# First norm's scale and shift spread by float32r products on four row groups, and one low weight part made on GpSimd

## The chip, the core and the metric

The kernel runs on one core of one Trainium2 chip. The metric is the device time of one launch in microseconds (us); lower is better. A core has five engines that work side by side and wait for one another by semaphores: TensorE (PE in the profile; PEld is its weight load), VectorE (DVE), ScalarE (ACT), GpSimd (POOL) and SyncE (SP), which here only issues transfers.

## What is computed

The reference is a trunk of two encoder layers over 512 tokens of width 1024. A layer norm stands ahead of the first layer, and the change is around that norm:

```python
def layer_norm(x, g, b):
    xf = x.astype(jnp.float32)
    mu = jnp.mean(xf, axis=-1, keepdims=True)
    var = jnp.mean(jnp.square(xf - mu), axis=-1, keepdims=True)
    return ((xf - mu) * lax.rsqrt(var + LN_EPS)).astype(x.dtype) * g + b
...
def hybrid_layer(x, w_in, ...):
    hcat = x @ w_in + b_in
    ...
    p_a = (y_a * jax.nn.silu(na_z)) @ w_br_a   # neighbourhood attention
    p_b = (y_b * jax.nn.silu(gq_z)) @ w_br_b   # grouped-query attention
    p_c = (y_c * jax.nn.silu(sg_z)) @ w_br_c   # spatial gating
    merged = g[:, :, 0] * p_a + g[:, :, 1] * p_b + g[:, :, 2] * p_c
    return layer_norm(DEEPNORM_ALPHA * x + merged @ w_out + b_out, ln_g, ln_b)
...
    h = layer_norm(x, ln_in_g, ln_in_b)
    for l in range(DEPTH):
        h = hybrid_layer(h, w_in[l], ...)
```

## The kernel before, in words

Tokens lie in four tiles of 128 rows. Every matrix product is made of three float32r products: each operand is split into a high part (a copy to float32r, on ScalarE) and a low part (the operand minus its high part), and high x high, low x high and high x low are summed in PSUM. Weights are split in the same way, 512 KB at a time.

`first_layer_start` (from L320) is the start of the program. It stands in `in_order`, which chains the instructions of each engine in the order in which they are written, so nothing in it is moved by a scheduler. Its work:

- SyncE issues the loads on its queue: token tile 0, weight parts q0 and q1, tile 1, q2, q3, tile 2, k0, tile 3, k1. Each is 512 KB. q0 to q3 are the query columns of the input projection (256 rows of depth each), k0 and k1 the key and value columns. Behind them come the constants (L99 to L104, L273 to L275).
- ScalarE's queue carries two loads: `lnrow`, the norm's scale g and shift b as one row of 2048 numbers on partition 0, and `ident`, the 64 KB identity for transposes.
- TensorE spreads that row over all partitions (L347): a column of ones on one partition times half a row of g or b gives a 128x512 tile in PSUM, once for each of g and b and each half, so four products in float32. The results are `gains[j, h]` (`lnb` in the profile; j is 0 for g, 1 for b; h the half).
- `stats(i)` makes a tile's mean and variance on VectorE (L223 to L225) and the power -0.5 on GpSimd (L226). `apply(i)` (L356) makes the normed tile in four VectorE steps, L359 and L361 for each half, then 4 + 4 transposes on TensorE (L365, `xt_in`), and ScalarE and VectorE split the transposed tile into `xh` and `xl` (L249, L250). Tile 0 reads `gains` from PSUM; the other tiles read `lnc`, ScalarE's copy of it in SBUF (L388).
- `high(n)` is a weight part's high copy on ScalarE (L337), `low(n, engine)` its low part on the named engine (L340): q0 and q1 on GpSimd, q2 and q3 on VectorE, k0 on GpSimd, k1 on VectorE.
- `gq_queries(0, i)` (L306) is the query product of tile i: 24 products, in six quartets. The first three quartets read q0 and q1 (high parts with `xh`, high with `xl`, low with `xh`), the last three q2 and q3 in the same way. `gq_keys_values(0, i)` (L196 to L198) follow from tile 0 on.

So the last quartet of `gq_queries(0, 0)` needs the low parts of q2 and q3; behind it on TensorE stand the transposes of tile 1, and behind them `gq_queries(0, 1)`.

After the start comes the planned part: a list of steps (`run_steps`) in which each projection's weights are loaded, split and used, up to the second layer's output.

Of the kernel before, what the change touches and what calls it, by code (L numbers as in the profile page):

```python
# [9 lines left out]
F32 = mybir.dt.float32  # L10
F32R = mybir.dt.float32r
AF = mybir.ActivationFunctionType
ALU = mybir.AluOpType
# [4 lines left out]
P = 128  # L18
D = 1024
KD = D // P  # L20
S = 512
# [31 lines left out]
def tile_encoder(ctx: ExitStack, tc: tile.TileContext, a, out):  # L53
    nc = tc.nc
    scalar = nc.scalar
# [14 lines left out]
    act = nc.scalar.activation  # L70
    dve = nc.vector
    pool = nc.gpsimd
    pe = nc.tensor

    cst = ctx.enter_context(tc.tile_pool(name="cst", bufs=1))
    wp = ctx.enter_context(tc.tile_pool(name="wp", bufs=2))
    rp = ctx.enter_context(tc.tile_pool(name="rp", bufs=8))
# [8 lines left out]
    pw = cst.tile([P, 10], F32, name="pw")  # L86
    pool.memset(pw, -0.5)

    one = cst.tile([P, 1], F32, name="one")
    pool.memset(one, 1.0)  # L90
    bcol = cst.tile([P, DEPTH, NCOL], F32, name="bcol")
    hcol = cst.tile([P, DEPTH, NCOL], F32, name="hcol")
    bvg = cst.tile([P, DEPTH, NKV], F32, name="bvg")
# [20 lines left out]
    def psum(tag, name):  # L114
        return pp.tile([P, S], F32, tag=tag, name=name, bufs=3 if tag == "acc" else 5)

    def t2(name):
        return tp.tile([P, S], F32, tag="t2", name=name, bufs=4)
# [4 lines left out]
    def asf(r):  # L123
        return r.bitcast(F32)
# [4 lines left out]
    def input_load(i):  # L129
        xi = st["xin", i] = t4(f"xin_{i}")  # L130
        nc.sync.dma_start(xi, a["x"][P * i:P * i + P, :])

    def load(src, nk, ncol, name):
        if name in ("gq0_0", "gq0_1", "gq0_2"):
            raw = fp.tile([P, nk, ncol], F32, tag="f8", name=f"raw_{name}")
        else:
            raw = wp.tile([P, nk, ncol], F32, tag="raw", name=f"raw_{name}", bufs=3)
        nc.sync.dma_start(raw, src.rearrange("(k p) c -> p k c", p=P))
        return raw
# [77 lines left out]
    def row_stats(src, n, name, wide=512):  # L217
        bs = sp.tile([P, 4, 6], F32, tag="st", name=f"st_{name}")
        mv = sp.tile([P, 2], F32, tag="mv", name=f"mv_{name}")
        rs = sp.tile([P, 1], F32, tag="rs", name=f"rs_{name}")  # L220
        nb = n // wide
        for j in range(nb):
            dve.bn_stats(bs[:, j, :], src[:, wide * j:wide * j + wide])  # L223
        dve.bn_aggr(mv, bs[:, 0:nb, :])
        dve.tensor_scalar(out=rs, in0=mv[:, 1:2], scalar1=LN_EPS, scalar2=None, op0=ALU.add)  # L225
        st["pow"] = pool.tensor_tensor(rs, rs, pw[:, 0:1], op=ALU.pow).ins  # L226
        return mv, rs
# [18 lines left out]
    def split_x(ps, i, b):  # L246
        pv = ps.rearrange("p (j t) -> p j t", t=P)
        hi = xh[:, 4 * b:4 * b + 4, P * i:P * i + P]
        act(hi, pv, AF.Copy)  # L249
        st["xl"] = dve.tensor_tensor(xl[:, 4 * b:4 * b + 4, P * i:P * i + P], pv, asf(hi), op=ALU.subtract).ins  # L250
# [37 lines left out]
    def gqw_tile(name):  # L288
        w = rp.tile([P, 2, 2, S], F32R, tag="r8", name=f"w_{name}")
        return w[:, 0], w[:, 1]  # L290
# [8 lines left out]
    def gq_queries(l, i):  # L299
        ps = st["psq", i] = psum("att", f"gq_{l}_{i}")  # L300
        tk = slice(P * i, P * i + P)
        w = [[st["gqw", k // 2][p][:, k % 2] for k in range(KD)] for p in range(2)]
        for k0 in range(0, KD, 4):
            for n, (x, p) in enumerate(((xh, 0), (xl, 0), (xh, 1))):
                for k in range(k0, k0 + 4):
                    pe.matmul(ps, lhsT=x[:, k, tk], rhs=w[p][k], start=n + k == 0, stop=n == 2 and k == KD - 1)  # L306

    def gq_keys_values(l, i):
        if i % 2 == 0:
            st["pskv", i // 2] = psum("acc", f"gkv_{l}_{i // 2}")  # L310
        ps = st["pskv", i // 2][:, 256 * (i % 2):256 * (i % 2) + 256]
        tk = slice(P * i, P * i + P)
        for k in range(KD):
            whi, wlo = st["kvw"][k // 4]
            mm3(ps, xh[:, k, tk], xl[:, k, tk], whi[:, k % 4], wlo[:, k % 4], k == 0, k == KD - 1)
# [3 lines left out]
    def first_layer_start():  # L319
        raw = {}  # L320
        input_load(0)
        rows = rp.tile([P, 2, D], F32, tag="r8", name="lnrow")[0:1]
        scalar.dma_start(rows, a["ln_in_rows"])
        scalar.dma_start(ident, a["ident"])
        for n in ("q0", "q1", 1, "q2", "q3", 2, "k0", 3, "k1"):
            if isinstance(n, int):
                input_load(n)
            else:
                raw[n] = load(*(gqw_spec if n[0] == "q" else kvw_spec)(0, int(n[1])))
        w = {}  # L330

        def high(n):
            if n[0] == "q":
                w[n] = gqw_tile(f"gq0_{n[1]}")
            else:
                w[n] = [wp.tile([P, 4, 256], F32R, tag=t, name=f"{t}_gkv0_{n[1]}") for t in ("whi", "wlo")]
            act(w[n][0], raw[n], AF.Copy)  # L337

        def low(n, engine):
            engine.tensor_tensor(w[n][1], raw[n], asf(w[n][0]), op=ALU.subtract)  # L340

        gains = {}
        lnc = st["lnc"] = cst.tile([P, 2, D], F32, tag="cvec", name="lnc_in")
        for h in range(2):
            for j in range(2):
                ps = gains[j, h] = psum("acc" if h + j < 2 else "att", f"lnb_{h}_{j}")
                pe.matmul(ps, lhsT=one[0:1].broadcast_to([1, P]), rhs=rows[:, j, 512 * h:512 * h + 512],  # L347
                          start=True, stop=True)

        def stats(i):  # L350
            st["stats", i] = row_stats(st["xin", i], D, f"in{i}")

        def apply(i):
            xi, (mv, rs) = st["xin", i], st["stats", i]
            xt = []
            for h in range(2):  # L356
                cs = slice(512 * h, 512 * h + 512)
                g, b = [gains[j, h] if i == 0 else lnc[:, j, cs] for j in range(2)]
                dve.scalar_tensor_tensor(out=xi[:, cs], in0=xi[:, cs], scalar=mv[:, 0:1], in1=g,  # L359
                                         op0=ALU.subtract, op1=ALU.mult)  # L360
                dve.scalar_tensor_tensor(out=xi[:, cs], in0=xi[:, cs], scalar=rs, in1=b, op0=ALU.mult, op1=ALU.add)  # L361
                ps = psum("att", f"xt_in{i}_{h}")
                for j in range(4):
                    c = 512 * h + P * j
                    pe.transpose(ps[:, P * j:P * j + P], xi[:, c:c + P], ident)  # L365
                xt.append(ps)
            for h in range(2):
                split_x(xt[h], i, h)
            if i:
                scalar.dma_start(hbuf[0][i], xi)  # L370

        stats(0)
        high("q0")
        low("q0", pool)
        high("q1")
        low("q1", pool)
        apply(0)
        high("q2")
        low("q2", dve)
        stats(1)  # L380
        high("q3")
        low("q3", dve)
        for kc in range(4):
            st["gqw", kc] = w[f"q{kc}"]
        gq_queries(0, 0)
        for h in range(2):
            for j in range(2):
                act(lnc[:, j, 512 * h:512 * h + 512], gains[j, h], AF.Copy)  # L388
        scalar.dma_start(hbuf[0][0], st["xin", 0])
        apply(1)  # L390
        high("k0")
        low("k0", pool)
        stats(2)
        high("k1")
        low("k1", dve)
        st["kvw"] = w["k0"], w["k1"]
        gq_queries(0, 1)
        gq_keys_values(0, 0)
        apply(2)
        stats(3)  # L400
        gq_keys_values(0, 1)
        gq_queries(0, 2)
        apply(3)
        gq_keys_values(0, 2)
        gq_keys_values(0, 3)
        gq_queries(0, 3)
# [514 lines left out]
    with in_order():  # L921
        first_layer_start()
# [4 lines left out]
    for l in range(DEPTH):  # L927
# [5 lines left out]
        M, R, T = gq_moments, gq_rotate, gq_stack  # L933
# [134 lines left out]
```

## Time and profile before

| | |
|---|---|
| median of 3 runs | 1092.2 us (1090.23 to 1094.16) |
| the profiled execution | 1090.98 us, of which the span in the trace is 1089.2 us |
| TensorE matmul busy | 1075.7 us (99% of the span), 5744 records |
| VectorE busy | 640.5 us (59%) |
| ScalarE busy | 470.6 us (43%) |
| GpSimd busy | 52.8 us (5%), 54 instructions |
| chain that ended last | PE 97%, DVE 2% |

The span begins with the first instruction that the trace holds; the 1.8 us between it and the execution's own time lie around it. Busy time is an average over the whole program. The change is in the first 25 us, so it is read from timelines and waits of that stretch.

### The profile page before, as it was taken

To read this page: it belongs to the slowest core of one execution; us is meant where nothing else is said; L and a number is where in the kernel's file an instruction comes from. 1 tells how busy PE (TensorE), PEld (TensorE's weight loads), DVE (VectorE), ACT (ScalarE), POOL (GpSimd) and SP (SyncE) were. 2 spreads that over 40 slices of the span, in tenths; PEclk is the share of its full clock that TensorE was granted. 3 is DMA by queue.
4 is the path that set the end of the run, shared out by engine and by line. 5 is a ranking of instruction groups with operands and counts; after the bars stand their busy time and mean duration, and the time that the engine had idled before them with its cause. 6 is when DMAs were issued, how large, how long until landed. Compare 5 with 4: busy or idle time off the path is not lost.

```text
span 1089.2 us, 14738 instructions
## 1 busy us (share of the span) xinstructions
PE 1075.7 (99%) x5744; PEld 887.8 (82%) x5744; DVE 640.5 (59%) x1205; ACT 470.6 (43%) x841; POOL 52.8 (5%) x54
## 2 busy tenths in 40 slices
PE   8999999999999999999999999999999999999997
PEld 5988788888888888888888887888888888888886
DVE  6775956665554543546876478566555555344465
ACT  4245735555655422334422365455645643223320
POOL 4420000000000000000021000000000000000001
PEclk9999999999999999999999999999999999999999
DMA  7522322213333433335652332222233334333421
GB/s 284 165 78 82 100 97 59 59 55 91 115 111 117 137 97 97 108 105 174 231 180 58 97 110 73 78 58 58 86 102 87 115 117 135 97 97 97 135 78 58
DMA packets 142808, 116.59 MB, mean 107 GB/s; under 512 B 4881, under 2 KB 130321, under 8 KB 142737
## 3 DMA queue, kind: packets, MB, share of 16 engines
q1 hardware_dynamic: 141872, 113.21, 33.5%
q10 hardware_dynamic: 866, 2.43, 0.6%
q8 instruction: 45, 0.74, 0.3%
q14 instruction: 25, 0.20, 0.1%
HBM read 109.34 MB, written 6.29 MB: 106 GB/s over the span
## 4 chain that ended last, share of the span: by engine, by line
PE 97%; DVE 2%; DMA 0%; issue 0%; ACT 0%; DVEq 0%
PE gq L306 4%; PE gy L735 3%; PE gb L196 3%; PE gc L198 3%; PE gc L197 3%; PE po L198 3%; PE po L197 3%; PE po L196 3%; PE gc L196 3%; PE ga L198 3%; PE ga L196 3%; PE gb L198 3%; PE gb L197 3%; PE ga L197 3%; PE gt L723 3%; PE gs L703 2%
## 5 line engine op out<-in xcount | busy, mean ns | idle before, releaser
L706 DVE TENSOR_REDUCE nm<-gs 128x1 f32<-128x512 f32 x64 | 42.3, 684 | 26.9 <-PE gs L704 26.8
L709 ACT ACTIVATE gp<-gs,nm 128x512 f32<-128x512 f32 x64 | 43.8, 688 | 21.4 <-DVE nm L706 19.8
L198 PE MATMUL gc<-xh,wlo_gc 128*128 128x512 f32 x128 | 51.1, 399 | 0.0
L725 ACT ACTIVATE gpT<-gt 128x512 f32<-128x512 f32 x64 | 36.7, 598 | 31.0 <-PE gt L723 30.8
L197 PE MATMUL gc<-xl,whi_gc 128*128 128x512 f32 x128 | 50.0, 391 | 0.0
L196 PE MATMUL gc<-xh,whi_gc 128*128 128x512 f32 x128 | 50.0, 391 | 0.0
L196 PE MATMUL gb<-xh,whi_gb 128*128 128x512 f32 x128 | 50.0, 391 | 0.0
L198 PE MATMUL gb<-xh,wlo_gb 128*128 128x512 f32 x128 | 49.8, 389 | 0.0
L197 PE MATMUL gb<-xl,whi_gb 128*128 128x512 f32 x128 | 49.8, 389 | 0.0
L196 PE MATMUL ga<-xh,whi_ga 128*128 128x512 f32 x128 | 49.8, 389 | 0.0
L198 PE MATMUL ga<-xh,wlo_ga 128*128 128x512 f32 x128 | 49.8, 389 | 0.0
L197 PE MATMUL ga<-xl,whi_ga 128*128 128x512 f32 x128 | 49.8, 389 | 0.0
L226 POOL TENSOR_TENSOR rs_po<-rs_po,pw 128x1 f32<-128x1 f32 x8 | 7.5, 939 | 814.4 <-DVE rs_po L225 814.4
L143 ACT ACTIVATE whi_gb<-raw_gb 128x1024 fp32r<-128x1024 f32 x16 | 17.0, 1060 | 60.4 <-PE pb L197 22.7
L779 ACT ACTIVATE nt<-nt,mx 128x256 f32<-128x256 f32 x64 | 30.1, 471 | 23.3 <-DVE mx L775 22.7
L144 DVE TENSOR_TENSOR wlo_ga<-raw_ga,whi_ga 128x1024 fp32r<-128x1024 f32 x16 | 19.6, 1222 | 33.5 <-ACT whi_ga L143 33.5
L735 PE MATMUL gy<-gpT,gv 128*64 128x128 f32 x512 | 38.8, 279 | 0.0
L723 PE MATMUL gt<-ident,gp 128*128 128x128 f32 x256 | 37.4, 276 | 0.7 <-ACT gpT L725 0.7
L735 PEld LDWEIGHTS gy<-gpT,gv 128*64 128x64 f32 x512 | 29.6, 136 | 10.2 <-issue 8.3
L144 DVE TENSOR_TENSOR wlo_gb<-raw_gb,whi_gb 128x1024 fp32r<-128x1024 f32 x16 | 19.6, 1222 | 30.1 <-ACT whi_gb L143 29.9
L723 PEld LDWEIGHTS gt<-ident,gp 128*128 128x128 f32 x256 | 29.7, 140 | 8.6 <-issue 2.7
L306 PE MATMUL gq<-w_gq,xh 128*128 128x512 f32 x128 | 34.0, 398 | 0.0
(282 smaller groups left out, 3099.0 us busy)
## 6 DMA issues: line engine op xcount, KB each, us to landing
raw_o<-in_w_out SPq DMA_DIRECT2D x24, 512.0 KB
raw_gc<-in_w_in SPq DMA_DIRECT2D x16, 512.0 KB
raw_gb<-in_w_in SPq DMA_DIRECT2D x16, 512.0 KB
raw_ga<-in_w_in SPq DMA_DIRECT2D x16, 512.0 KB
raw_gq<-in_w_in SPq DMA_DIRECT2D x8, 512.0 KB
raw_sv<-in_w_in SPq DMA_DIRECT2D x8, 512.0 KB
raw_nv<-in_w_in SPq DMA_DIRECT2D x8, 512.0 KB
raw_zb<-in_w_in SPq DMA_DIRECT2D x8, 512.0 KB
```

Of the source, the lines that this page charges most:

```text
L144: dve.tensor_tensor(wlo, raw, asf(whi), op=ALU.subtract)
L196: pe.matmul(ps, lhsT=lhi, rhs=rhi, start=first, stop=False)
L197: pe.matmul(ps, lhsT=lhi, rhs=rlo, start=False, stop=False)
L198: pe.matmul(ps, lhsT=llo, rhs=rhi, start=False, stop=last)
L306: pe.matmul(ps, lhsT=x[:, k, tk], rhs=w[p][k], start=n + k == 0, stop=n == 2 and k == KD - 1)
L703: pe.matmul(ps, lhsT=lhs, rhs=st["ks"][:, g, 0, :], start=True, stop=False)
L706: dve.tensor_reduce(out=nm, in_=ps, axis=AX.X, op=ALU.max, negate=True)
L709: act(pt, ps, AF.Exp, bias=nm, accum_out=sm)
L723: pe.transpose(ps[:, P * k:P * k + P], pt[:, P * k:P * k + P], ident)
L725: act(pT, ps, AF.Copy)
L735: pe.matmul(ps[64 * e:64 * e + 64, P * t:P * t + P], lhsT=st["gv"][:, k, HD * g:HD * g + HD], rhs=st["gp", hp, t, e][:, P * k:P * k + P], ...
L779: act(T[:, cs], T[:, cs], AF.Exp, bias=mx[:, i:i + 1], scale=SCALE, accum_out=sm[:, i:i + 1])
```

## The change

The scale and shift no longer come as one row. A transfer (`lnflat`) writes them to all 128 partitions: a row of 512 numbers to each, the same one to 32 partitions in a row, in the order g first half, b first half, g second half, b second half. The input array is laid out anew on the host for that. ScalarE makes the high part of this tile, GpSimd the low part, and a 32x128 block of 1/32 takes the place of the column of ones. Each `gains[j, h]` is now two float32r products (high, then low) over the 32 partitions that hold its row, so eight products in place of four. The block of 1/32 is filled by a GpSimd memset in the same tile. The second edit makes the low part of q3 on GpSimd in place of VectorE, and puts it ahead of `stats(1)` in the text.

```diff
-    one = cst.tile([P, 1], F32, name="one")
-    pool.memset(one, 1.0)
...
         raw = {}
         input_load(0)
-        rows = rp.tile([P, 2, D], F32, tag="r8", name="lnrow")[0:1]
-        scalar.dma_start(rows, a["ln_in_rows"])
+        rows = rp.tile([P, 3, S], F32R, tag="r8", name="lnrow")
+        one = rows[:, 2, 0:P]
+        pool.memset(asf(one), 1.0 / 32)
+        R = a["ln_in_rows"]
+        flat = t2("lnflat")
+        scalar.dma_start(flat, bass.AP(tensor=R.tensor, offset=R.offset, ap=[[S, 4], [0, 32], [1, S]]))
         scalar.dma_start(ident, a["ident"])
...
         lnc = st["lnc"] = cst.tile([P, 2, D], F32, tag="cvec", name="lnc_in")
-        for h in range(2):
-            for j in range(2):
-                ps = gains[j, h] = psum("acc" if h + j < 2 else "att", f"lnb_{h}_{j}")
-                pe.matmul(ps, lhsT=one[0:1].broadcast_to([1, P]), rhs=rows[:, j, 512 * h:512 * h + 512],
-                          start=True, stop=True)
+        act(rows[:, 0], flat, AF.Copy)
+        pool.tensor_tensor(rows[:, 1], flat, asf(rows[:, 0]), op=ALU.subtract)
+        for p in range(2):
+            for h in range(2):
+                for j in range(2):
+                    q = 64 * h + 32 * j
+                    if p == 0:
+                        gains[j, h] = psum("acc" if h + j < 2 else "att", f"lnb_{h}_{j}")
+                    pe.matmul(gains[j, h], lhsT=one[q:q + 32], rhs=rows[q:q + 32, p],
+                              start=p == 0, stop=p == 1)
...
         high("q2")
         low("q2", dve)
+        high("q3")
+        low("q3", pool)
         stats(1)
-        high("q3")
-        low("q3", dve)
...
-    arrays["ln_in_rows"] = np.ascontiguousarray(np.stack([v["ln_in_g"], v["ln_in_b"]])[None])
+    arrays["ln_in_rows"] = np.ascontiguousarray(np.stack([v["ln_in_g"], v["ln_in_b"]]).reshape(2, 2, S).transpose(1, 0, 2))
```

Of the rest of the program no engine's order is different. Two places move.

GpSimd, from its first memset to the low part of k0, before (`rs_in` is the power of `stats`, `w_gq` the low parts of q0, q1, q3, `wlo_gkv` that of k0):

```order
L87 MEMSET pw 128x10
L90 MEMSET one 128x1
L109 MEMSET nkl 64x512 x2
L226 ISA
L226 TENSOR_TENSOR rs_in_136<-rs_in_136,pw 128x1
L340 TENSOR_TENSOR w_gq_0_142<-raw_gq_0_107,w_gq_0_142 128x1024
L340 TENSOR_TENSOR w_gq_1_145<-raw_gq_1_109,w_gq_1_145 128x1024
L226 TENSOR_TENSOR rs_in_171<-rs_in_171,pw 128x1
L340 TENSOR_TENSOR wlo_gkv_0_230<-raw_gkv_0_119,whi_gkv_0_229 128x1024
```

The same place on GpSimd after the change:

```order
L87 MEMSET pw 128x10
L109 MEMSET nkl 64x512 x2
L324 MEMSET lnrow 128x128
L349 ISA
L349 TENSOR_TENSOR lnrow<-lnflat,lnrow 128x512
L226 TENSOR_TENSOR rs_in_142<-rs_in_142,pw 128x1
L344 TENSOR_TENSOR w_gq_0_148<-raw_gq_0_107,w_gq_0_148 128x1024
L344 TENSOR_TENSOR w_gq_1_151<-raw_gq_1_109,w_gq_1_151 128x1024
L344 TENSOR_TENSOR w_gq_3_175<-raw_gq_3_115,w_gq_3_175 128x1024
L226 TENSOR_TENSOR rs_in_180<-rs_in_180,pw 128x1
L344 TENSOR_TENSOR wlo_gkv_0_236<-raw_gkv_0_119,whi_gkv_0_235 128x1024
```

The low part of the norm's rows now stands ahead of tile 0's power, and the low part of q3 ahead of tile 1's power.

VectorE, from the last step of `apply(0)` to the first of `apply(1)`, before (`lnb` is `gains`, `lnc_in` its copy in SBUF):

```order
L361 SCALAR_TENSOR_TENSOR xin_102<-xin_102,rs_in_136,lnb_1_132 128x512
L250 TENSOR_TENSOR xl<-xt_in_0_150,xh 128x4x128
L250 TENSOR_TENSOR xl<-xt_in_1_157,xh 128x4x128
L340 TENSOR_TENSOR w_gq_2_166<-raw_gq_2_113,w_gq_2_166 128x1024
L223 BN_STATS st_in_169<-xin_111 128x6 x2
L224 BN_AGGR mv_in_170<-st_in_169 128x2
L225 TENSOR_SCALAR rs_in_171<-mv_in_170 128x1
L340 TENSOR_TENSOR w_gq_3_177<-raw_gq_3_115,w_gq_3_177 128x1024
L359 SCALAR_TENSOR_TENSOR xin_111<-xin_111,mv_in_170,lnc_in 128x512
```

The same place on VectorE after the change:

```order
L370 SCALAR_TENSOR_TENSOR xin_100<-xin_100,rs_in_142,lnb_1_134 128x512
L250 TENSOR_TENSOR xl<-xt_in_0_156,xh 128x4x128
L250 TENSOR_TENSOR xl<-xt_in_1_163,xh 128x4x128
L344 TENSOR_TENSOR w_gq_2_172<-raw_gq_2_113,w_gq_2_172 128x1024
L223 BN_STATS st_in_178<-xin_111 128x6 x2
L224 BN_AGGR mv_in_179<-st_in_178 128x2
L225 TENSOR_SCALAR rs_in_180<-mv_in_179 128x1
L368 SCALAR_TENSOR_TENSOR xin_111<-xin_111,mv_in_179,lnc_in 128x512
```

One row is gone from VectorE: q3's low part between the statistics of tile 1 and the first step of `apply(1)`.

## Rows read from the trace of the kernel before

**Rows 1.** Waits of TensorE over the whole span: us in total, times, longest.

```profile
PE lnb L347 <- DMA lnrow<-in_ln_in_rows: 3.5, 1, 3.5
PE xt_in L365 <- DVE xin L361: 1.8, 2, 0.9
```

**Rows 2.** Chain that ended last, 0 to 60 us: start us, us, what.

```profile
0.72 2.67 DMA lnrow<-in_ln_in_rows
...
3.53 7.16 PE lnb L347 x8
...
14.26 1.23 DVE w_gq L340
...
17.04 1.23 DVE w_gq L340
...
20.57 0.76 DVE xin L361
...
22.10 5.49 PE gq L306 x24
```

**Rows 3.** Timeline of TensorE: start us, us, instruction, shapes, count, [idle before].

```profile
12.42 1.80 PE L306 MATMUL gq<-w_gq,xh 128*128 128x512 f32 x4
14.06 1.09 PE L306 MATMUL gq<-w_gq,xl 128*128 128x512 f32 x4
14.98 2.00 PE L306 MATMUL gq<-w_gq,xh 128*128 128x512 f32 x8
...
19.86 0.66 PE L365 MATMUL xt_in<-ident,xin 128*128 128x128 f32 x4 [0.81 <-DVE xin L361]
```

**Rows 4.** Timeline of VectorE.

```profile
4.70 1.29 DVE L223 BATCH_NORM_STATS2 st_in<-xin 128x6 f32<-128x512 f32 x2 [4.70 <-DMA xin<-in_x]
6.33 0.74 DVE L359 SCALAR_TENSOR_TENSOR xin<-xin,mv_in,lnb 128x512 f32<-128x512 f32 x1
10.72 0.75 DVE L361 SCALAR_TENSOR_TENSOR xin<-xin,rs_in,lnb 128x512 f32<-128x512 f32 x1 [0.96 <-PE lnb L347]
25.01 2.24 DVE L340 TENSOR_TENSOR wlo_gkv<-raw_gkv,whi_gkv 128x1024 fp32r<-128x1024 f32 x1
```

**Rows 5.** Timeline of ScalarE.

```profile
6.17 1.06 ACT L337 ACTIVATE w_gq<-raw_gq 128x1024 fp32r<-128x1024 f32 x1 [3.21 <-DMA raw_gq<-in_w_in]
7.44 1.06 ACT L337 ACTIVATE w_gq<-raw_gq 128x1024 fp32r<-128x1024 f32 x1 [0.22 <-DMA raw_gq<-in_w_in]
11.77 0.60 ACT L249 ACTIVATE xh<-xt_in 128x512 fp32r<-128x512 f32 x1 [3.27 <-PE xt_in L365]
13.18 2.00 ACT L337 ACTIVATE w_gq<-raw_gq 128x1024 fp32r<-128x1024 f32 x2
```

**Rows 6.** Timeline of GpSimd.

```profile
6.57 0.56 POOL L226 TENSOR_TENSOR rs_in<-rs_in,pw 128x1 f32<-128x1 f32 x1 [4.56 <-DVE rs_in L225]
7.30 4.66 POOL L340 TENSOR_TENSOR w_gq<-raw_gq,w_gq 128x1024 fp32r<-128x1024 f32 x2 [0.18 <-ACT w_gq L337]
17.19 1.48 POOL L226 TENSOR_TENSOR rs_in<-rs_in,pw 128x1 f32<-128x1 f32 x1 [5.23 <-DVE rs_in L225]
23.76 2.40 POOL L340 TENSOR_TENSOR wlo_gkv<-raw_gkv,whi_gkv 128x1024 fp32r<-128x1024 f32 x1 [5.09 <-ACT whi_gkv L337]
```

**Rows 7.** DMA view, 0 to 8 us: packets in all, and queue 10 (ScalarE's): packets, MB, share.

```profile
DMA packets 1011, 2.24 MB, mean 281 GB/s; under 512 B 75, under 2 KB 203, under 8 KB 1010
q10 hardware_dynamic: 146, 0.07, 4.0%
```

**Rows 8.** DMA view, 236 to 248 us: packets in all, and of SyncE's queue.

```profile
DMA packets 1102, 1.26 MB, mean 105 GB/s; under 512 B 79, under 2 KB 1101, under 8 KB 1101
q1 hardware_dynamic: 1101, 1.24, 34.6%
```

**Rows 9.** Timeline of SyncE's queue: the transfers issued in that stretch.

```profile
236.00 0.37 SPq L138 DMA_DIRECT2D raw_pc<-in_w_br_c  x1
236.41 9.44 SPq L691 DMA_DIRECT2D rpb<-in_rpb  x8
```

## The prediction

> **What bounds the kernel now.** I read the waits of TensorE first: in the whole span they hold two entries of over a microsecond, 3.5 us for the norm's row and 1.8 us for VectorE at the transposes of tile 1 [rows 1]. So whatever TensorE starts late in the first 22 us is added to the end, and nothing behind it can take it back: the transposes of tile 1 end at 22.10 us and `gq_queries(0, 1)` runs on from there [rows 2]. The question is only when that point comes.
>
> The chain says what leads to it [rows 2]: the row lands at 3.39 us, its four float32 products take 7.16 us, VectorE makes the low parts of q2 and q3 (1.23 us each), and the last step of `apply(1)` ends at 21.33 us. The timelines fill it in. On VectorE, tile 0 lands at 4.70 us and its statistics end at 6.33; the last step of `apply(0)` waits for a product and ends at 11.47 us [rows 4]. From there to the low part of q2 at 14.26 us it is 2.79 us (transposes, two ScalarE copies, high part of q2). The low part of q3 ends at 18.27 us and `apply(1)` needs 21.33 - 18.27 = 3.06 us for its four steps [rows 2].
>
> **How long two-operand work on VectorE and GpSimd takes side by side.** The low part of k1 takes VectorE 2.24 us, against 1.23 us for the same size in the chain [rows 2, 4]. GpSimd was making the low part of k0 from 23.76 to 26.16 us [rows 6], and VectorE's ends 27.25 us, 1.09 after that. The power on GpSimd takes 0.56 us alone and 1.48 us beside VectorE's low part of q3; it ends at 18.67 us, 0.40 after that part [rows 2, 6]. I read this as: when both read two SBUF operands, one stands still until the other is done.
>
> **Edit 2, the low part of q3 on GpSimd.** It takes 1.23 us off VectorE, in the chain. But GpSimd needs 2.33 us for one part (two in 4.66 us [rows 6]) and can begin only when VectorE's low part of q2 is done. The statistics of tile 1 (4.70 to 6.33 for tile 0, so 1.6 us [rows 4]) go on beside it, but the first step of `apply(1)` reads two SBUF operands and waits: 2.33 us behind q2's low part instead of 1.6 + 1.23 = 2.83. Behind it stands the power of tile 1, which ends 0.4 us after that step; so the second step waits some 0.3 us more than before. Gain: 2.83 - 2.33 - 0.3 = **0.2 us**, not 1.23. The memset of 128x128 lies in GpSimd's idle time ahead of 6.57 us [rows 6] and costs nothing there, unless it were to last past the landing of `lnflat`.
>
> **Edit 1, the products.** Removed: 7.16 us of float32 products. Added: a transfer of 256 KB in place of 8 KB; one ScalarE copy of 128x512, 0.60 us [rows 5]; one GpSimd subtraction of 128x512, between the 0.56 us of a one-column operation and 2.33 us for 1024 columns [rows 6], I take 1.2, half of the latter, being its half; eight products. A 512-column float32r product costs 0.41 us at the pace of the first quartet (14.06 - 12.42 = 1.64 us for four) and 0.23 us at that of the second (0.92 us) [rows 3]: the 1.2 GHz and the 2.4 GHz level. At the slow pace the four high products end 1.64 us after the copy, behind the subtraction or with it, and the first low one is out some 0.8 us later. From landing to the first usable gain: 0.6 + 0.1 + 1.64 + 0.7, that is **3.0 us**. The next products come every 0.41 us, faster than VectorE's steps (0.75 us), so whether the four row groups run at once decides little. `apply(0)` then runs without a wait: 3.06 us.
>
> **When the transfer lands** is the unknown that decides. Bounds: the 8 KB row lands at 3.39 us [rows 2]; if it shared all engines evenly with tile 0, it would land with tile 0 at about 4.7 us [rows 4]. But the source pattern in the diff has four pieces outermost, each read 32 times. What do rows show of such patterns? On ScalarE's queue `ident` has 128 rows and `lnrow` one; 146 packets [rows 7] are 128 + 1 of data and 17 more, and one packet of all has over 8 KB: I read 16 small ones for `ident` and a single one for `lnrow`, one for each DMA engine used. At 236 us there go one weight load (512 rows, 16 engines) and eight `rpb` transfers (64 rows each, source with 8 pieces outermost) [rows 9]: 1024 rows, and 79 small packets [rows 8], near 16 + 8 x 8 = 80 and far from 16 x 9 = 144. So a transfer is spread over as many engines as its outermost count allows: 1, 8, 128 rows over 16. With 4, `lnflat` lies on four engines, 64 KB on each. The Trainium skill states this ("DMA: Bandwidth & Descriptors", section "Why a DMA increments its semaphore by 16 and not by 1"): a transfer uses the largest number up to 16 that divides both sides' outermost sizes, here 4 of 4 and 128. No run here shows a transfer with four yet. By the rule the sum is the one below, by sixteen engines it is that of rival 2.
>
> A 512 KB load puts 32 KB on each engine and lands 1.27 us behind the one before it (7.44 - 6.17 [rows 5]). So 64 KB are two such slots. If `lnflat` is served ahead of tile 0, it lands near 4.70 + 1.27 = 6.0 us and tile 0 at 7.2; if they alternate in slots, at 7.2; if tile 0 and q0 both pass first or between, 4.70 + 3 x 1.27 = 8.5. I take **7.5 us**, near the middle. Everything behind it on SyncE's queue comes up to 2.5 us later on those four engines.
>
> **The sum**, from the landing at 7.5 us: first gain at 10.5, `apply(0)` done at 13.6 (before: 11.47), so +2.1 us. GpSimd: subtraction done near 9.4, tile 0's power 10.0, low parts of q0 and q1 (high copies from about 8 and 10) at 14.7 (before 11.96). They are wanted by the third quartet, which starts some 2.6 us after the first one (1.64 + 0.92), now at about 14.5 + 2.6; this covers them, and there is nothing left to cover it if GpSimd is over 2 us later still. Low part of q2 at 14.26 + 2.1 = 16.4 to 17.6; q2's load, by 1.27 us a load three behind q0, lands by 10.0 + 2.5, in time. GpSimd's low part of q3 to 19.95; `apply(1)` from there with 0.3 us of the power: 23.3 (before 21.33). The query products of tile 0, 14.5 + 1.64 + 5 x 0.92 = 20.7, are done by then. Edit 1 costs 2.1, edit 2 gives some 0.1 to 0.2 back: **+2.0 us**. Against the profiled execution, 1090.98, that is 1093.0; it lies 1.2 below the median of the runs, so on the median I forecast 1092.2 + 2.0 = **1094.2 us**.
>
> **Rivals.**
> 1. *`lnflat` first on its four engines.* Lands near 6.0; tile 0's statistics then end at 7.2 + 1.63 = 8.9, and the first gain at 9.0: `apply(0)` at 12.1, +0.6, less edit 2: +0.4, 1092.6 us. For it: ScalarE issues at 0.72 us, as early as SyncE. Against: nothing in the rows gives that queue precedence. Chance 0.13.
> 2. *Not slower: sixteen engines after all.* Landing at 4.7, first gain at 7.7, `apply(0)` at 10.8: -0.7, with edit 2 -0.9; with the 3.39 us of the small row, -2.2. Time 1091.3 us, down to 1090.0. Decides below a landing of some 5.6 us. For it: 128 destination rows, as the full-speed loads have; against: the packet counts. Chance 0.13.
> 3. *TensorE's clock stays low.* The rise came between the first and second quartet, after 7.16 us of products and the transposes in a row [rows 2, 3]; the granted clock in the profile's slices reads full throughout, so only the pace tells. Now eight short products stand in place of that stretch, with idle time around them. If all of `gq_queries(0, 0)` goes at 0.41 us, it ends at 14.5 + 24 x 0.41 = 24.3, and with two sets of transposes (0.66 us [rows 3]) the next starts at 25.6, against 22.10: +3.5, 1095.7 us, and 0.72 us for each slow quartet more. Up to three slow quartets cost nothing, since TensorE waits for `apply(1)` anyway; from the fourth on it decides. The Trainium skill ("TensorE: Matmul & The Clock Gate", Part 1) says that the gate opens on recent activity and that idle stretches close it, which would speak for this; no run here shows the gate closing, and the 1.8 us of waits at tile 1 did not. Chance 0.12.
>
> **How the numbers follow.** The forecast has 0.62. About 0.3%, 3.3 us, is what a measurement of this kernel can tell from no change; the three runs shown spread 3.9 us. Slower by over that: most of rival 3 (0.09) and the forecast's upper end, a landing at 8.5 us (+3.0) with the runs' spread (0.08): 0.17. Faster: only the lowest end of rival 2 with the spread, 0.03. Within: 0.80. The range leaves out the slow tail of rival 3 and the low end of rival 2: 1090.6 to 1096.4. What is likeliest alone, a landing at 7.2 to 8.5, gives 1093.9 to 1095.2.
>
> **What would show it.** In the changed profile: ScalarE's copy to `lnrow` waits for `lnflat` until about 7.5 us (right), or is over by 5.3 (rival 2); q0's high part starts over 1 us later than 6.17; VectorE's first step on `lnb` starts near 10.5; the first step of `apply(1)` starts when GpSimd's low part of q3 ends; `gq_queries(0, 1)` starts near 24.1 in place of 22.10, and TensorE has no new wait after it. Wrong would be: a copy that starts before 5.6 us, or a difference after 25 us.

## The result, and the profile after

The changed kernel takes 1097.28 us (median of 6 runs, 1097.0 to 1100.56), the kernel before beside it 1091.32 us: a ratio of 1.0056, 95% interval 1.0040 to 1.0072. It is slower, by 6.0 us where 2.0 were forecast, and above the range.

TensorE's waits after the change, over the whole span (us in total, times, longest); the first two answer to [rows 1]:

```profile
PE lnb L356 <- ACT lnrow L348: 11.9, 1, 11.9
PE xt_in L374 <- DVE xin L370: 2.9, 3, 1.7
PE gt L732 <- ACT gpT L734: 1.2, 2, 0.7
PE lnb L356 <- POOL lnrow L349: 0.5, 1, 0.5
```

The first wait has grown from 3.5 to 11.9 us, while the products behind it have shrunk from 7.16 us to two sets of 0.8. The third entry stood at 0.7 us before; it lies near 120 us, in a part of the program that the change does not touch.

The chain of the changed kernel, 0 to 60 us (start us, us, what), beside [rows 2]:

```profile
0.72 10.41 DMA lnflat<-in_ln_in_rows
...
11.86 1.29 POOL lnrow L349
13.20 0.84 PE lnb L356 x2
14.03 0.75 DVE xin L368
...
16.42 0.76 DVE xin L370
...
18.97 1.90 ACT w_gq L341 x2
20.94 1.93 POOL w_gq L344
...
25.95 0.76 DVE xin L370
...
27.48 5.49 PE gq L306 x24
```

The transfer lands at 0.72 + 10.41 = 11.13 us. `gq_queries(0, 1)` starts at 27.48 us in place of 22.10: 5.38 us later. The span is 6.5 us longer (1095.7 against 1089.2), so another 1.1 us is lost behind it. I call that part the *late shift*: the shift of the span less the shift of `gq_queries(0, 1)`.

Timelines of the changed kernel, ScalarE and then GpSimd, VectorE, TensorE (columns as in [rows 3]):

```profile
0.72 1.15 ACTq L327 DMA_DIRECT2D lnflat<-in_ln_in_rows  x1
11.15 0.63 ACT L348 ACTIVATE lnrow<-lnflat 128x512 fp32r<-128x512 f32 x1 [7.56 <-DMA lnflat<-in_ln_in_rows]
...
11.86 1.28 POOL L349 TENSOR_TENSOR lnrow<-lnflat,lnrow 128x512 fp32r<-128x512 f32 x1 [9.75 <-ACT lnrow L348]
...
20.94 2.50 POOL L344 TENSOR_TENSOR w_gq<-raw_gq,w_gq 128x1024 fp32r<-128x1024 f32 x1 [2.66 <-ACT w_gq L341]
...
4.36 1.29 DVE L223 BATCH_NORM_STATS2 st_in<-xin 128x6 f32<-128x512 f32 x2 [4.36 <-DMA xin<-in_x]
14.02 0.75 DVE L368 SCALAR_TENSOR_TENSOR xin<-xin,mv_in,lnb 128x512 f32<-128x512 f32 x1 [7.95 <-PE lnb L356]
...
22.72 1.26 DVE L368 SCALAR_TENSOR_TENSOR xin<-xin,mv_in,lnc_in 128x512 f32<-128x512 f32 x1
...
17.99 2.06 PE L306 MATMUL gq<-w_gq,xh 128*128 128x512 f32 x4
19.84 1.91 PE L306 MATMUL gq<-w_gq,xl 128*128 128x512 f32 x4
...
26.85 0.63 PE L374 MATMUL xt_in<-ident,xin 128*128 128x128 f32 x4 [0.74 <-DVE xin L370]
```

Tile 0 lands earlier than before (4.36 us, before 4.70), so `lnflat` was not served ahead of it. VectorE then stands still for 7.95 us until the first gain is there. The first step of `apply(1)` (22.72 us) takes 1.26 us in place of 0.75, beside GpSimd's low part of q3, which ends at 23.44. Two quartets of tile 0's query products run at the slow pace, and TensorE still waits 0.74 us for VectorE at the end.

The late landing also holds back SyncE, whose load of tile 2 is issued at 11.15 us in place of 4.07; its wait in the first 30 us:

```profile
SPq L131 <- DMA lnflat<-in_ln_in_rows: 7.3, 1, 7.3
```

No compute engine waits for tile 2 afterwards, so this costs nothing.

### The profile page after: what moved, and what is told of

It reads as the page before. It is cut to its first block, busy times and chain, and to the rows that moved or that the text cites. A ratio compares the mean times of both kernels' runs of the same rounds, so it can differ in the third digit from the quotient of the medians.

```text
span 1095.7 us, 14740 instructions
## 1 busy us (share of the span) xinstructions
PE 1071.7 (98%) x5744; PEld 887.1 (81%) x5744; DVE 640.0 (58%) x1204; ACT 470.8 (43%) x842; POOL 55.4 (5%) x56
## 4 chain that ended last, share of the span: by engine, by line
PE 95%; DVE 2%; DMA 2%; POOL 0%; ACT 0%; issue 0%; DVEq 0%; POOLq 0%; ACTq 0%
PE gq L306 3%; PE gy L744 3%; PE gb L196 3%; PE gc L197 3%; PE po L198 3%; PE gc L196 3%; PE po L197 3%; PE po L196 3%; PE gc L198 3%; PE gb L197 3%; PE ga L196 3%; PE ga L197 3%; PE gb L198 3%; PE ga L198 3%; PE gt L732 3%; PE gs L712 1%
```

## The experiments

"Before" and "after" are the kernels before and after the change. Ratios are to runs of the kernel before on the same chip (medians 1090.89 to 1091.10 us).

### The landing

Theory 1: four pieces outermost in the source pattern put the transfer on four DMA engines, which is what makes it late. Theory 2: the repeated reading of one source row does. Three edits of the pattern keep 256 KB and 2 KB a partition; the input array is laid out to match.

e1_sixteen (each row four times in the source) and e2_eight (twice):

```diff
-ap=[[S, 4], [0, 32], [1, S]]
+ap=[[S, 16], [0, 8], [1, S]]
```

```diff
-ap=[[S, 4], [0, 32], [1, S]]
+ap=[[S, 8], [0, 16], [1, S]]
```

> The same 256 KB, the same copies and products; only the source array holds each of the four rows four times, so that the pattern has 16 pieces outermost, each read 8 times. Theory 1 (the transfer lies on as many DMA engines as its source has outermost pieces): on 16 engines it lands at 4.7 to 5.4 us in place of 11.1, VectorE's first step on the gains starts near 8.0, the query products of tile 1 start 21.2 to 21.6 us (before 22.10, after 27.48); time about 0.6 us under the kernel before, ratio 0.999. Theory 2 (reading one row many times is slow, whatever the engines): still 8 us or later, query products of tile 1 later than 24 us, ratio 1.002 or more.

> The same with each row held twice: 8 pieces outermost, each read 16 times. Theory 1: half the work on each engine, so about half the way from 1.9 us to the landing: near 7 us; query products of tile 1 at about 23.4 us. Theory 2: 9 us or later.

e3_four_distinct (33 copies of each row, none read twice, four outermost as in the change):

```diff
-ap=[[S, 4], [0, 32], [1, S]]
+ap=[[33 * S, 4], [S, 32], [1, S]]
```

> Again 4 pieces outermost, but each of the 128 rows is read from a place of its own (the source holds every row 33 times, the pattern takes 32 of them). Theory 1: no difference from the changed kernel, landing at 10.5 to 11.5 us, query products of tile 1 near 27.5. Theory 2: the landing comes at 7 us or earlier, query products of tile 1 before 24 us.

The chains, first e1, then e2, then e3:

```profile
0.72 5.05 DMA lnflat<-in_ln_in_rows
...
22.12 5.49 PE gq L306 x24
```

```profile
0.72 6.92 DMA lnflat<-in_ln_in_rows
...
23.99 5.49 PE gq L306 x24
```

```profile
0.72 10.07 DMA lnflat<-in_ln_in_rows
...
27.15 5.49 PE gq L306 x24
```

Landings 5.77, 7.64 and 10.79 us. Theory 1 holds, theory 2 falls: without a repeated row the transfer is 0.3 us faster, with 16 engines 5.4. The packet records bear out the number of engines: at most 5 packets of the transfer run at a time in the changed kernel and 6 in e3, but 10 in e2 and 19 in e1, a little above four, eight and sixteen. The rule that the prediction took from the Trainium skill ("DMA: Bandwidth & Descriptors", section "Why a DMA increments its semaphore by 16 and not by 1") agrees with these landings. The landings and starts of e1 and e2 came 0.4 to 0.6 us behind what was expected.

One number comes back in every kernel with the products of the change and edit 2: from the landing to `gq_queries(0, 1)` it is 27.48 - 11.13 = 16.35 us after the change, 22.12 - 5.77 = 16.35 in e1, 16.35 in e2, 16.36 in e3. The start of the program hangs on the landing alone. The times: e1 1092.64 us, ratio 1.0019 (1.0008 to 1.0030); e2 1093.95, e3 1097.16 (one run each, before 1091.06).

e6_queue_ahead (the transfer of the change on SyncE's queue, ahead of tile 0):

```diff
+        nc.sync.dma_start(flat, bass.AP(...))
         input_load(0)
...
-        scalar.dma_start(flat, bass.AP(...))
```

> The changed transfer, still 4 pieces outermost, put on SyncE's queue ahead of token tile 0, so that it does not take turns with the loads. Theory 1 with turns (half of the 9 us on the four engines belonged to the loads of the other queue): it lands at 5.5 to 7.0 us and tile 0 some 1.3 to 2 us behind its 4.4; query products of tile 1 at 22 to 23.5. If the four engines are slow on this transfer by themselves, without turns: 10 us or later, tile 0 later still, query products of tile 1 past 27.

e6's timelines of ScalarE and VectorE, and its chain:

```profile
7.51 0.63 ACT L348 ACTIVATE lnrow<-lnflat 128x512 fp32r<-128x512 f32 x1 [5.10 <-DMA lnflat<-in_ln_in_rows]
...
8.59 1.29 DVE L223 BATCH_NORM_STATS2 st_in<-xin 128x6 f32<-128x512 f32 x2 [8.59 <-DMA xin<-in_x]
```

```profile
23.84 5.50 PE gq L306 x24
```

Ahead of tile 0 the transfer still lands only at 7.49 us, between the two outcomes that I had set against each other, and tile 0 at 8.59. Going first takes 3.6 us off the way from issue to landing (6.77 us in place of 10.41), sixteen engines 5.4. 1093.88 us (one run). `gq_queries(0, 1)` is again 16.35 us behind the landing.

e7_small (8 KB into four partitions of a tile that GpSimd has set to zero):

```diff
+    lnflat = tp.tile([P, S], F32, tag="t2", name="lnflat", bufs=4)
+    pool.memset(lnflat, 0.0)
...
-        pool.memset(asf(one), 1.0 / 32)
+        pool.memset(asf(one), 1.0)
...
-        flat = t2("lnflat")
+        flat = lnflat
-        scalar.dma_start(flat, bass.AP(..., ap=[[S, 4], [0, 32], [1, S]]))
+        scalar.dma_start(flat[0:P:32], bass.AP(..., ap=[[S, 4], [1, S]]))
```

> The changed kernel without the wide transfer: the flat tile is set to zero by GpSimd, the 8 KB go into four partitions, one in each row group, and the block of ones holds 1.0 in place of 1/32. If the transfer is the whole loss and the products are as cheap as the changed kernel showed (about 2.9 us from landing to the first step on a gain): landing near 4.0 us, first step near 6.9, apply(0) done near 10.1, gq_queries(0, 1) near 20.4, 1.7 us earlier than before; the time 0.7 to 1.7 us below that of the kernel before (up to 1 us of what comes later in the kernel with sixteen engines may come here too), ratio 0.9985 to 0.9994. Rival: TensorE's granted clock, which rises at 13.76 us in the kernel before, does not rise earlier here, and the first quartets at the low level take the gain back: gq_queries(0, 1) at 21.5 or later, ratio 0.9995 or above.

e7's chain:

```profile
1.27 4.56 DMA lnflat<-in_ln_in_rows
...
22.19 5.48 PE gq L308 x24
```

A miss: 8 KB land at 5.83 us, hardly ahead of the 256 KB of e1. The memset holds the issue until 1.27 us, the issue takes 1.11 us, and the four packets (84 ns each) start only at 4.91 us, after most of tile 0's. The size was not the price; by the trace, the late issue and the late turn of its packets were. Ratio 1.0009 (1.0001 to 1.0018).

### Edit 2

e4_part_only (edit 2 alone on the kernel before, as below) and e8_small_rows_only (e7 with the same edit undone):

```diff
         low("q2", dve)
-        stats(1)
         high("q3")
-        low("q3", dve)
+        low("q3", pool)
+        stats(1)
```

> Edit 2 alone on the kernel before: the low part of q3 on GpSimd, statistics of tile 1 behind it. My theory (two-operand work of VectorE and GpSimd takes turns, and tile 1's power on GpSimd stands behind the first step of apply(1)): gq_queries(0, 1) starts at 21.8 to 21.9 us in place of 22.10, ratio about 0.9998. Rival (the part is simply off VectorE): 1.23 us earlier, near 20.9, ratio 0.9989.

> The kernel of e7_small with the low part of q3 on VectorE again, behind the statistics of tile 1 (edit 2 undone). My theory: edit 2 is worth 0.2 to 0.3 us here too, gq_queries(0, 1) near 20.7 us, ratio 0.9987 to 0.9996. Rival: the part is worth its 1.23 us: near 21.6.

e8's chain:

```profile
1.27 4.43 DMA lnflat<-in_ln_in_rows
...
22.35 5.50 PE gq L308 x24
```

e8 needs 22.35 - 5.70 = 16.65 us from the landing, e7 16.36: edit 2 is worth 0.3 us there, not 1.23. In e4 `gq_queries(0, 1)` starts 1.43 us earlier than before, but the 8 KB row landed 1.12 us earlier in that execution (2.27 us against 3.39), which leaves 0.3 as well. Ratios 0.9998 (0.9989 to 1.0006) for e4, 1.0015 (1.0007 to 1.0024) for e8.

### The late shift

e1, e2, e3, e6, e7 and e8 have a late shift of 1.05 to 1.25 us, e4 one of -0.1. So it belongs to edit 1, and not to a late start: e1 and e7 start `gq_queries(0, 1)` within 0.1 us of before. Edit 1 also removed a constant of 128x1, and with it 32 bytes a partition at the bottom of SBUF: all tiles laid out later stand 32 bytes lower, off a multiple of 64. And `lnflat` takes a turn in the ring t2, so each later tile of that ring, the `rpb` tiles among them, stands in another of its four buffers.

e10_after_aligned (the 32 bytes put back), e11_before_shifted (32 more bytes in the kernel before) and e15_aligned_no_ring (e10 with `lnflat` in the tile `lnc_in`, so that every tile has its old address):

```diff
+    pad = cst.tile([P, 1], F32, name="pad")
+    pool.memset(pad, 1.0)
```

and in e15 also

```diff
-        flat = t2("lnflat")
+        flat = lnc[:, 0, 0:S]
```

> The changed kernel with a constant of 128x1 (32 bytes of SBUF a partition) put back where the old block of ones stood. Theory A (the removed constant moves every tile behind it by 32 bytes, off a multiple of 64, and transfers into such tiles take longer): the first 27 us as in the changed kernel, gq_queries(0, 1) near 27.5 us, but no further shift behind it: span 5.4 us above that of the kernel before in place of 6.5, ratio about 1.0046. Theory B (the rest comes from the changed order of the first 27 us or from the other rotation of the lnflat ring): span 6.5 above, ratio 1.0056.

> The kernel before with a second constant of 128x1, 32 bytes more in front of all later tiles, nothing else. Theory A: nothing changes up to 110 us, then the same steps of 0.3, 0.15, 0.3 and 0.15 us near 120, 230 to 360, 653 and 700 to 750 us; about 1.0 us in all, ratio 1.0009. Theory B: ratio 1.0000 and no steps.

> The changed kernel with the 32 bytes put back and lnflat placed in the tile lnc_in, which is not in use yet, in place of the ring t2, so that every tile has the address of the kernel before. gq_queries(0, 1) near 27.1 us as in the changed kernel and e10. If the rest of the late shift (0.45 us in e10) comes from the ring t2 that lnflat turned by one tile: no shift behind 27 us over 0.1 us, and a span 0.4 us closer to the shift of gq_queries(0, 1) than in e10. If it comes from the later start itself: 0.3 to 0.5 us again.

| kernel | tiles 32 bytes off | ring turned | `gq_queries(0, 1)` | span | late shift |
|---|---|---|---|---|---|
| before | no | no | 22.10 | 1089.2 | 0 |
| e4 | no | no | 20.67 | 1087.7 | -0.1 |
| e15 | no | no | 26.93 | 1093.9 | -0.1 |
| e11 | yes | no | 22.20 | 1089.9 | 0.6 |
| e10 | no | yes | 27.05 | 1094.8 | 0.65 |
| after | yes | yes | 27.48 | 1095.7 | 1.1 |

The two addresses make the late shift, about half each, and with both old addresses it is gone although the start is 4.8 us late. (The 32 bytes alone, theory A of e10 and e11, make half of it.) Set product against product, the changed kernel falls behind by 0.3 us near 120 us, by 0.2 between 125 and 230, by 0.25 near 655 and by 0.2 between 660 and 800; e4 and e15 stay within 0.05 us of the kernel before from 45 us on. The first of these steps lies at the relative-position bias. ScalarE's copy of `rpb` there, with its wait, before, after, in e11 and in e15:

```profile
118.30 0.44 ACT L692 ACTIVATE bm<-rpb 128x256 f32<-128x256 f32 x1 [1.08 <-DMA rpb<-in_rpb]
```

```profile
124.13 0.43 ACT L701 ACTIVATE bm<-rpb 128x256 f32<-128x256 f32 x1 [1.46 <-DMA rpb<-in_rpb]
```

```profile
118.71 0.44 ACT L694 ACTIVATE bm<-rpb 128x256 f32<-128x256 f32 x1 [1.31 <-DMA rpb<-in_rpb]
```

```profile
123.03 0.44 ACT L701 ACTIVATE bm<-rpb 128x256 f32<-128x256 f32 x1 [1.01 <-DMA rpb<-in_rpb]
```

In moved tiles the transfers land 0.2 to 0.4 us later behind their issue, ScalarE's later copies follow, and TensorE waits for them at `gt` (0.31 us before, 0.73 after). In time the whole is small: e10 1.0044 (1.0032 to 1.0056), e15 1.0042 (1.0030 to 1.0054), and e11's 1.0003 (0.9994 to 1.0012) alone would not have told it from nothing; the traces do. Why a transfer into a moved tile takes longer stays open: the median packet of `rpb` takes the same time in both. Nor is it shown that the other steps are transfers too. Each entry of the table rests on one execution. e13 and e14, which have the 32 bytes but turn another ring, show 0.3 to 0.35 us of late shift too.

### Another order, and a version that beats both

e9_small_reordered takes the rows of e7, puts `stats(1)` right behind tile 0's vector steps, and the two halves of `apply(1)` around the low part of q3, on VectorE again (`vector` is the two VectorE steps of a half, `turn` its transposes, `copy` ScalarE's copies to `lnc`). e12_reordered_aligned is e9 with the 32 bytes.

```diff
-        apply(0)
+        xt = []
+        for h in range(2):
+            vector(0, h)
+            xt.append(turn(0, h))
+        stats(1)
+        for h in range(2):
+            split_x(xt[h], 0, h)
         high("q2")
         low("q2", dve)
+        copy(0)
         high("q3")
-        low("q3", pool)
-        stats(1)
+        copy(1)
+        vector(1, 0)
+        low("q3", dve)
+        vector(1, 1)
...
```

> The rows of e7_small and another order in place of edit 2: the statistics of tile 1 right behind tile 0's vector steps, so that its power on GpSimd stands beside nothing on VectorE that reads two SBUF operands; the copies of the gains to SBUF around the high part of q3, and the two halves of apply(1) ahead of and behind the low part of q3, on VectorE. If the turns and the power's place behind them are what made edit 2 worth so little: gq_queries(0, 1) at 19.3 to 19.8 us, about 2.5 us earlier than before, ratio 0.9970 to 0.9985. If TensorE itself is the limit (tile 0's query products end at its own pace): not below 20.4.

> The kernel of e9_small_reordered with the same 32 bytes put back. Theory A: gq_queries(0, 1) near 20.9 us as there, and no later shift: about 1.1 us below e9, ratio 0.9990 to 0.9995. Theory B: as e9, ratio 1.0004.

e9's chain:

```profile
12.93 6.84 PE gq L308 x24
19.77 0.45 PE xt_in L376 x4
...
20.89 5.78 PE gq L308 x24
```

`gq_queries(0, 1)` starts at 20.89 us, not 19.3 to 19.8, mostly since the rows land at 5.73 us and not near 4.0. From the landing it is 15.16 us in place of 16.36: the order gives 1.2 us. The chain now runs through TensorE itself, whose first query products go at the slow pace. e9 1.0004 (0.9996 to 1.0012), e12 0.9992 (0.9983 to 1.0000). Their profiled executions lie 1.5 us apart: e12's late shift is 1.25 us smaller (0.25 in place of 1.5), and it starts `gq_queries(0, 1)` 0.28 us earlier, with one slow quartet of tile 0 in place of two. So it is the 32 bytes again, but not they alone.

e13_single_row keeps the one 8 KB row of the kernel before, splits it on one partition, and makes eight products of one row each, in the order of e9 and with the 32 bytes in place; e14_single_row_pool moves its fourth low part to GpSimd.

```diff
+        scalar.dma_start(flat, a["ln_in_rows"])
...
+        def part(engine, g):
+            engine.tensor_tensor(lo[:, g], flat[:, g], asf(hi[:, g]), op=ALU.subtract)
...
+        for g in range(4):
+            act(hi[:, g], flat[:, g], AF.Copy)
+        part(dve, 0)
+        part(pool, 1)
...
         stats(0)
+        part(pool, 2)
+        product(2)
...
+        vector(0, 0)
+        xt = [turn(0, 0)]
+        part(dve, 3)
+        product(3)
+        vector(0, 1)
...
```

and e14 against e13

```diff
         stats(0)
-        part(pool, 2)
-        product(2)
+        for g in 2, 3:
+            part(pool, g)
+            product(g)
...
         vector(0, 0)
         xt = [turn(0, 0)]
-        part(dve, 3)
-        product(3)
         vector(0, 1)
```

> A version for speed: the 8 KB stay one row on one partition, as in the kernel before (landing 2.3 to 3.4 us), and are split there into four high parts (ScalarE) and four low parts (VectorE, GpSimd, GpSimd, VectorE) of 512 columns; eight float32r products of one row each; the order of e9 behind them and the 32 bytes in place. If the landing is what held e7 to e9 back: first step of apply(0) near 6.5 us, its last one done near 10.0 (11.47 before), gq_queries(0, 1) at 19.0 to 19.8, 2.3 to 3.1 us earlier than before, ratio 0.9972 to 0.9982. If TensorE's granted clock, which rises later where the long products are gone, is the limit: gq_queries(0, 1) not below 20.4, ratio 0.9985 or above.

> The kernel of e13_single_row with the fourth low part on GpSimd, ahead of the low parts of q0 and q1, in place of VectorE. If what held e13 back is only that VectorE's 512-column subtraction (5.63 us) stood still until GpSimd had made both low parts: last step of apply(0) at 10.2 to 11.0 us (14.69 in e13), gq_queries(0, 1) at 19.3 to 20.4 us (24.15 in e13; 22.10 before), ratio 0.9973 to 0.9985. Rival: the low parts of q0 and q1, now 1.3 us later on GpSimd, come too late for the third quartet, or the clock rises late: gq_queries(0, 1) at 20.9 or later, ratio 0.9988 or above.

e13, VectorE and GpSimd:

```profile
3.65 0.68 DVE L347 TENSOR_TENSOR lnlo<-lnflat,lnhi 1x512 fp32r<-1x512 f32 x1 [3.65 <-ACT lnhi L355]
...
7.43 5.63 DVE L347 TENSOR_TENSOR lnlo<-lnflat,lnhi 1x512 fp32r<-1x512 f32 x1
...
6.64 1.26 POOL L347 TENSOR_TENSOR lnlo<-lnflat,lnhi 1x512 fp32r<-1x512 f32 x1
7.86 4.65 POOL L341 TENSOR_TENSOR w_gq<-raw_gq,w_gq 128x1024 fp32r<-128x1024 f32 x2
```

The same subtraction takes 0.68 us alone and 5.63 beside GpSimd: it begins while GpSimd's own subtraction runs (6.64 to 7.90 us), and it ends 0.55 us after *both* of the low parts that GpSimd makes next. e13 is slower, 1.0025 (1.0015 to 1.0034). The Trainium skill ("SBUF — State Buffer", section "Who interferes with whom") says that a VectorE instruction with two SBUF inputs contends with a GpSimd instruction that reads SBUF, for a port pair that one holds at a time. The trace agrees and adds that VectorE got no turn between GpSimd's instructions in a row.

e14 sets that right; its VectorE, then its chain:

```profile
10.42 0.75 DVE L370 SCALAR_TENSOR_TENSOR xin<-xin,rs_in,lnb 128x512 f32<-128x512 f32 x1 [0.48 <-PE lnb L352]
```

```profile
20.28 5.49 PE gq L306 x24
```

`apply(0)` is done at 11.17 us (11.47 before, and 10.2 to 11.0 expected) and `gq_queries(0, 1)` starts 1.82 us earlier than before, from a row that lands at about 3.4 us in both. 1089.74 us against 1090.89, ratio 0.9987 (0.9978 to 0.9996): faster than both kernels, by a little. That is not shown to be the float32r products' doing: `apply(0)` is done only 0.3 us earlier, and the rest of the 1.82 us follows behind it, where the new order has taken the statistics of tile 1 (1.6 us) out of the way between the low parts of q2 and q3. No run has the new order with the products of the kernel before.

## Why the prediction was wrong

The sum has two wrong terms and one that was nearly right. In us: forecast +2.0; landing +3.6 too early; the way from the landing 0.25 too long; late shift +1.1 not foreseen. 2.0 + 3.6 - 0.25 + 1.1 = 6.45, and the span shows 6.5.

- **"I take 7.5 us" for the landing failed: 11.1 measured**, and the upper bound of 8.5 failed with it. That four engines carry 64 KB each was right. What failed is the price "64 KB are two such slots" of 1.27 us, taken from full-speed loads. The packets, from the trace: they start at 3.44 us, with tile 0's first (3.57), 1.6 us after the end of an issue that takes 1.15 us, not the 0.53 us of the single row. They end at 10.34 us, so the transfer is spread over 6.9 us, all beside SyncE's loads. An engine carries 32 packets, of 123 ns on the mean, 3.9 us: by this estimate it gave a little over half of its time to `lnflat`. And 2 KB packets of *both* queues took about 120 ns in that stretch, where before 84 are usual. No two starts of `lnflat` packets lie more than 0.28 us apart, so the two queues shared the four engines over the whole stretch. Turns packet by packet would fit that, but the records do not name a packet's engine, and why packets get longer there stays open.
- **From the landing on** the working held. First step on a gain 14.02 - 11.13 = 2.9 us behind the landing (forecast 3.0), `apply(0)` done 6.05 (6.1), `apply(1)` done 15.6 (15.8), `gq_queries(0, 1)` 16.35 (16.6).
- **Edit 2, "0.2 us, not 1.23":** 0.3 by e7 and e8. Two-operand work that takes turns was the right reading of [rows 2, 4, 6], shown plainly by e13. The first step of `apply(1)` in the changed kernel is done only 0.5 us after GpSimd's low part of q3, as forecast.
- **"A difference after 25 us" was to prove me wrong, and did.** I had taken the removed constant for nothing. It moved later tiles by 32 bytes, and `lnflat` turned the ring t2, a term that the sum did not have; shown by e4, e10, e11 and e15. The forecast of "up to 2.5 us" for what stands behind the transfer on SyncE's queue failed as well: the issue of tile 2 came 7.1 us later, at no cost.
- **Rival 1** (first on its engines) fell: tile 0 landed at 4.36 us. **Rival 2** (sixteen engines) was wrong for the change, and e1, which makes it true, shows that it would not have been a gain: landing 5.77 us, just beyond the 5.6 from which it was to decide, and 1.0019.
- **Rival 3** (the clock): by the pace two quartets of tile 0 ran at the slow level in place of one, and it cost nothing, since TensorE waited for VectorE behind them all the same; "up to three slow quartets cost nothing" fits. In e9, where VectorE is no longer late, the slow quartets stand in the chain.

## What to carry to other kernels

Before a small early transfer is made wide, count the DMA engines that its outermost dimension gives it and what shares them: here 256 KB on four engines beside the first loads landed 7.7 us after the 8 KB row. Hold against every saving what must land first: a start that hangs on one landing moves with it one to one. After an edit that adds or drops even a tiny tile, look for shifts far behind the edit, and put the addresses back before you explain them otherwise.

## What was not expected of the hardware

- Moving all later tiles by 32 bytes of SBUF shifted the later part of this program by 0.6 us (e11), by 1.1 us with the turned ring; `rpb` transfers into the moved tiles landed 0.2 to 0.4 us later.
- A 512-column VectorE subtraction of 0.68 us stood still for 5 us until GpSimd had ended three instructions in a row.
- The same 8 KB packet took 1433 ns in the profiled execution of before, 1545 in e11 and 1412 in e14, and 342 and 327 in e4 and e13; the landing moves by 1.1 us between executions, at the head of everything.
- Four products of 32 rows each, on four row groups, ran in 0.80 us together, while one 512-column product takes 0.41 us at that pace: they do overlap, though no term needed it.
